# Ten pairs of projection tasks as block products with seven multiplications of blocks

## The chip, the cores and the metric
The kernel runs on one core of a Trainium2 chip. The metric is the device time of one execution in microseconds (us); lower is better. The engines are named as the profile names them: PE (TensorE, matmuls), PEld (its weight loads), DVE (VectorE), ACT (ScalarE), POOL (GpSimd) and SP (SyncE, which issues most of the DMAs). Each takes its instructions in order from a queue of its own.

## The reference
One step of a decoder layer for a prompt of 512 positions and 8 samples of 4 positions each, 544 columns in all (T), with a width of 1024.

```python
proj = jnp.einsum('btd,de->bte', x, p['w_in']) + p['b_in']
(q, k, v_a, o_a, z_a, i_pre, f_pre, u_b, v_b, z_b, x_c, z_c,
 g_a, g_b, g_c) = jnp.split(proj, _split_points(), axis=-1)
...
vn = layer_norm(v_b, p['gmlp_ln_g'], p['gmlp_ln_b'])
y_b = chunk_spatial_gate(u_b, vn, p['gmlp_ws'], p['gmlp_bs']) * jax.nn.silu(z_b)
...
merged = (jax.nn.sigmoid(g_a) * (y_a @ p['w_proj_a'])
          + jax.nn.sigmoid(g_b) * (y_b @ p['w_proj_b'])
          + jax.nn.sigmoid(g_c) * (y_c @ p['w_proj_c']))
out = merged @ p['w_out']
x_new = layer_norm(ALPHA * x + out, p['ln_g'], p['ln_b'])
```

y_a comes from four heads with a matrix memory, y_c from a gated linear recurrence (a scan over the positions). The change touches g_a, g_c and v_b.

## The kernel before
**Tasks.** Every projection is cut into tasks of 128 output channels (`proj`, `add`, run by `project`, L301). A task holds a 1024 x 128 block of weights as eight k-tiles of 128 x 128. The operands are fp32, and a matmul takes fp32r, so each operand is split into a high part (an ACT copy to fp32r) and a low part (a DVE subtraction): wh and wl for the weights (`need`, L255), xh and xl for the input. `products` adds wh·xh, wh·xl and wl·xh; T = 544 columns are two halves of 272, each in a PSUM bank of its own. A task is thus 8 x 3 x 2 = 48 matmuls. Its evacuation from PSUM is a function (`evac`): for the gates ga, gc one ACT tanh of 544 columns (gta, gtc), for pa a DVE multiplication by the gate that makes the merged sum mg, for vb an ACT copy with bias (vbt).

**Order.** The list of tasks is: the heads; xc0, zc0 to xc7, zc7 (the recurrence's inputs); ga0, ga1, pa0, pa1, ga2, ga3, pa2 and so on to pa7; the same with gc and pc; vb0 to vb7; zb0 to zb7; u0 to u7; gb and pb; then the output projection. PE, ACT, DVE and POOL take their instructions in the order in which the program records them. Work beside the tasks (the attention, the recurrence, `parts` which splits y_a into ya*h and ya*l for pa, `mixers`, `norm_v`) is written as generators: each yields a time or the name of something it waits for, and `poll`, called between groups of matmuls, lets each go on whose time has come by `clk`, a count of matmul time kept while recording. `force` drives them until a name in `gates` is done. So the recurrence of channel block 7 (tg7, a7, m7, the scan into xcv7, z_zc7) is recorded among the matmuls of ga0 to pa1, and `mixers` (nnps, lvps, lvo: states that go out, and masks) starts at vb1. `norm_v` transposes the finished vbt tiles into vt0, vt1 and so on for the layer norm.

**Buffers.** PSUM is split into `mm` (two buffers of two banks, the tasks' accumulators), `m2` (one buffer of two banks: lg, lvps, vt) and `aux` (two of one bank). A task's accumulator is free again when its `evac` has run. The weights wait in `wr` (two buffers of two tasks each, 1 MB, loaded from SP's queue), wh and wl have three buffers each.

Of the kernel before, what the change touches and what calls it, by code (L numbers as in the profile page):

```python
# [15 lines left out]
P = 128  # L16
# [25 lines left out]
def kernel(  # L42
# [227 lines left out]

    def products(i, k, ps):
        wh, wl = wts[i]
        vh, vl = tasks[i][4]()
        for n, (a, b) in enumerate(((wh, vh[k]), (wh, vl[k]), (wl, vh[k]))):
            for hf in range(2):
                matmul(ps[:, hf, :HT], a[:, k, :], b[:, hf * HT:(hf + 1) * HT],
                       start=(k == 0 and n == 0), stop=(k == KT - 1 and n == 2))
            if n < 2:
                poll()

    def project(first, last):
        for i in range(at[first], at[last] + 1):
# [3 lines left out]
            for _ in need(i):  # L286
                pass
            for _ in need(i + 1):
                pass
# [13 lines left out]
            poll()  # L303

# [92 lines left out]
    hrows = dr.tile([H, 2 * T + NS], F32, name="hrows")  # L397
    r_int = cp.tile([P, NS], F32, name="r_int")
# [166 lines left out]
    def add_head(h):  # L565
# [73 lines left out]
    def attention(h):  # L639
# [6 lines left out]
        bc = sp.tile([P, T + NS], F32, tag="bc", name=f"bc{h}", bufs=1)  # L646
# [62 lines left out]
        qp = sp.tile([P, 2, NS], F32, tag="qp", name=f"qp{h}", bufs=1)  # L709
# [44 lines left out]
        qt = sp.tile([P, 2, NS], F32, tag="qt", name=f"qt{h}", bufs=1)  # L754
# [77 lines left out]
        for dk in range(2):  # L832
# [8 lines left out]
            t_ = sp.tile([P, 258], F32, tag="cpo", name=f"cpo{h}{dk}", bufs=1)  # L841
# [171 lines left out]
    def add_merge(off, w, key, y):  # L1013
# [10 lines left out]
        vec = lambda: ([a for a, _ in ys], [b for _, b in ys])  # L1024

# [16 lines left out]

        for c in range(0, KT, 2):
# [11 lines left out]

    def ev_vb(c):
        def evac(ps):
            vbt[c] = slot("qk", f"vbt{c}")
            A.activation(h2(vbt[c]), p2(ps), AF.Identity, bias=bcol(O_VB + c * P)[0])
            if c == KT - 1:  # L1060
                go(norm_v())
        return evac
# [35 lines left out]
    def mixers():  # L1098
# [7 lines left out]
        nnr = sp.tile([P, 512], F32, tag="c0", name="nnr", bufs=4)[:36, :DK]  # L1106
# [9 lines left out]
        for hf in range(2):  # L1116
            t_ = sp.tile([P, 512], F32, tag="c0", name=f"lvo{hf}", bufs=4)
# [23 lines left out]
        mx.update(wmt=wmt, wsm2=wsm2, bsb=bsb)  # L1141

# [12 lines left out]
    def norm_v():  # L1155
        lng, lnb = [], []
        for hf in range(2):
            a = sp.tile([P, 512], F32, tag="c0h", name=f"glg{hf}", bufs=2)
            b = sp.tile([P, 512], F32, tag="c0l", name=f"glb{hf}", bufs=2)
# [5 lines left out]
        for i in range(NCH + 1):  # L1165
# [10 lines left out]
            for hf in range(2):  # L1176
                t_ = slot("kv", f"vn{i}{hf}") if i < NCH else sp.tile([P, 512], F32, tag="c0", name=f"vn{i}{hf}", bufs=4)
# [42 lines left out]
    def output():  # L1220
# [25 lines left out]
        for hf in range(2):  # L1246
# [6 lines left out]
            for oi, i in enumerate(orders[hf]):  # L1253
# [24 lines left out]
                if i == NCH:  # L1278
                    lo = sp.tile([P, 512], F32, tag="c0l", name=f"outl{hf}", bufs=2)
# [68 lines left out]
    gates["u0"] = ("vn",)  # L1348
# [6 lines left out]
    output()  # L1355
    assert not gens
# [30 lines left out]
```

## Time and profile before

| | us |
|---|---|
| median of 3 runs | 988.69 (984.44 to 989.75) |
| the profiled execution, its own time | 987.27 |
| its span, first to last instruction | 985.5 |
| PE busy | 972.1 (99%) |
| DVE busy | 549.8 (56%) |
| ACT busy | 412.3 (42%) |
| POOL busy | 97.5 (10%) |

The granted clock of PE was 0.992 of full speed on average. All times of the trace count from the start of the span. Ends of matmuls are modelled, so the time of one is read from the distance of many starts, as in the chain of waits, and not from the duration of one.

### The profile page before, as it was taken

The numbers are of one execution on the slowest core, as the hardware profiler recorded it, in microseconds if no ns is written. First come the engines' busy times: TensorE is split into PE (matmuls) and PEld (weight loads), VectorE is DVE, ScalarE is ACT, GpSimd is POOL, SyncE is SP. The second block draws the span as 40 slices with busy tenths as digits, with TensorE's granted clock in tenths as the row PEclk, the third lists the DMA queues.
The fourth block names the chain that finished last, engine by engine and source line by source line (L and its number), as shares of the span: only waits on it lengthen the run. The fifth ranks groups of instructions, "written<-read, shape, count | busy, mean of one in ns | idle before, by whom it ended". The sixth has DMA issues, their size and how long they took to land.

```text
span 985.5 us, 17775 instructions
## 1 busy us (share of the span) xinstructions
PE 972.1 (99%) x7433; PEld 948.7 (96%) x7433; DVE 549.8 (56%) x897; ACT 412.3 (42%) x653; POOL 97.5 (10%) x210
## 2 busy tenths in 40 slices
PE   8999999999999999999999999999999999999996
PEld 8999999999999999999999999999999999999975
DVE  4665675666567568889932243333167545433456
ACT  4454445445444545989922232222233213322421
POOL 5122002201200220001000000000000000000204
PEclk9999999999999999999999999999999999999998
DMA  8323721641462263233222222232223313431322
GB/s 252 101 63 120 214 80 61 192 131 50 133 195 86 60 195 105 77 96 92 87 86 88 91 84 95 95 109 70 88 84 97 102 63 99 140 107 43 102 65 101
DMA packets 101968, 103.55 MB, mean 105 GB/s; under 512 B 5358, under 2 KB 95320, under 8 KB 101888
## 3 DMA queue, kind: packets, MB, share of 16 engines
q1 hardware_dynamic: 100352, 101.46, 33.3%
q8 instruction: 58, 0.95, 0.4%
q10 hardware_dynamic: 640, 0.66, 0.2%
q0 software_dynamic: 896, 0.31, 0.1%
q14 instruction: 22, 0.18, 0.1%
HBM read 90.40 MB, written 12.00 MB: 104 GB/s over the span
## 4 chain that ended last, share of the span: by engine, by line
PE 98%; DMA 1%; issue 0%; ACT 0%; POOL 0%; DVE 0%; ACTq 0%; POOLq 0%
PE ps_v L96 5%; PE out L96 5%; PE ps_u L96 5%; PE ps_z L96 5%; PE ps_q L96 5%; PE ps_vb L96 5%; PE ps_zc L96 5%; PE ps_xc L96 5%; PE ps_pa L96 5%; PE ps_zb L96 5%; PE ps_ga L96 5%; PE ps_pc L96 5%; PE ps_k L96 5%; PE ps_o L96 5%; PE ps_gc L96 5%; PE ps_gb L96 5%
## 5 line engine op out<-in xcount | busy, mean ns | idle before, releaser
L795 DVE SCALAR_TENSOR_TENSOR c<-c,bc,cs 128x512 f32<-128x512 f32 x32 | 23.9, 746 | 36.2 <-PE cs L96 35.8
L777 POOL TENSOR_SCALAR wvm<-wvt,bm 96x256 fp32r<-96x256 f32 x32 | 31.5, 987 | 87.4 <-PE cs L96 87.4
L96 PE MATMUL ps_v<-xh,wh_v 128*128 128x272 f32 x128 | 29.1, 310 | 0.0
L774 ACT ACTIVATE c0h<-c 128x512 fp32r<-128x512 f32 x32 | 20.0, 625 | 21.6 <-DMA c<-in_state_mlstm_c_dram 20.1
L96 PE MATMUL ps_v<-xl,wh_v 128*128 128x272 f32 x128 | 28.1, 303 | 0.0
L96 PE MATMUL ps_v<-xh,wl_v 128*128 128x272 f32 x128 | 27.7, 299 | 0.0
L96 PE MATMUL ps_q<-xh,wh_q 128*128 128x272 f32 x128 | 27.3, 294 | 0.0
L96 PE MATMUL ps_u<-xh,wh_u 128*128 128x272 f32 x128 | 27.3, 294 | 0.0
L96 PE MATMUL ps_o<-xl,wh_o 128*128 128x272 f32 x128 | 27.1, 293 | 0.0
L96 PE MATMUL ps_z<-xh,wl_z 128*128 128x272 f32 x128 | 26.9, 291 | 0.0
L96 PE MATMUL ps_zb<-xh,wh_zb 128*128 128x272 f32 x128 | 26.8, 291 | 0.0
L96 PE MATMUL ps_o<-xh,wl_o 128*128 128x272 f32 x128 | 26.8, 291 | 0.0
L96 PE MATMUL ps_vb<-xh,wh_vb 128*128 128x272 f32 x128 | 26.8, 290 | 0.0
L96 PE MATMUL ps_z<-xh,wh_z 128*128 128x272 f32 x128 | 26.7, 290 | 0.0
L96 PE MATMUL ps_q<-xh,wl_q 128*128 128x272 f32 x128 | 26.7, 290 | 0.0
L96 PE MATMUL ps_q<-xl,wh_q 128*128 128x272 f32 x128 | 26.7, 289 | 0.0
L96 PE MATMUL ps_xc<-xl,wh_xc 128*128 128x272 f32 x128 | 26.6, 289 | 0.0
L96 PE MATMUL ps_gc<-xh,wh_gc 128*128 128x272 f32 x128 | 26.6, 288 | 0.0
L96 PE MATMUL ps_k<-xh,wl_k 128*128 128x272 f32 x128 | 26.6, 289 | 0.0
L96 PE MATMUL ps_gb<-xl,wh_gb 128*128 128x272 f32 x128 | 26.5, 289 | 0.0
L96 PE MATMUL ps_vb<-xh,wl_vb 128*128 128x272 f32 x128 | 26.5, 288 | 0.0
L96 PE MATMUL ps_zc<-xh,wh_zc 128*128 128x272 f32 x128 | 26.5, 289 | 0.0
(774 smaller groups left out, 3280.6 us busy)
## 6 DMA issues: line engine op xcount, KB each, us to landing
c<-in_state_mlstm_c_dram SPq DMA_DIRECT2D x32, 256.0 KB
out_dram<-c SPq DMA_DIRECT2D x32, 256.0 KB
wr_q<-in_w_in_dram SPq DMA_DIRECT2D x8, 512.0 KB
wr_k<-in_w_in_dram SPq DMA_DIRECT2D x8, 512.0 KB
wr_o<-in_w_in_dram SPq DMA_DIRECT2D x8, 512.0 KB
wr_z<-in_w_in_dram SPq DMA_DIRECT2D x8, 512.0 KB
wr_xc<-in_w_in_dram SPq DMA_DIRECT2D x8, 512.0 KB
wr_zc<-in_w_in_dram SPq DMA_DIRECT2D x8, 512.0 KB
```

Source lines behind the costliest of these rows:

```text
L96: PE.matmul(out, a, b, start=start, stop=stop)
L774: A.activation(hi[:, :512], t_[:, :512], AF.Copy)
L777: G.tensor_scalar(wvm, f(wvs), bm[:, b:b + 1], None, op0=ALU.mult)
L795: V.scalar_tensor_tensor(t_[:, :512], t_[:, :512], inter[:, DS * b + DS - 1:DS * b + DS], ps, op0=ALU.mult, op1=ALU.add)
```

## The change
ga4 to ga7, gc0 to gc7 and vb0 to vb7 are taken in pairs of neighbouring tasks, ten in all. A pair multiplies a 1024 x 256 block of weights with the 1024 x 544 input. `seven` sees it as 2 x 2 blocks: of the weights by halves of the k-tiles and by task, of the input by halves of the k-tiles and of the columns. It forms the four result blocks from seven block products (Winograd's form) in place of eight, each of 4 k-tiles, 3 parts and 272 columns: 84 matmuls in place of 96. The products go to three PSUM areas: X (four products), Y (two) and Z (one). `factors` makes the weights' block sums on DVE and splits them; `token_sums` makes the input's block sums once, from the time of ga0 on: t2, t3 and t4 into new tiles (40 DVE and 12 ACT operations of 128x272), and t1, after ga3, in place of one quarter of x (16 and 4). The quarter is saved to DRAM before (`spill`, eight DMAs of 139 KB) and brought back by `restore` after the last product that uses t1, in vb6. ga0 to ga3 and all other tasks stay as they were. `mixers` starts at zb0 and no longer at vb1; `norm_v` starts when the last vb pair ends. Small tiles move to a pool (`top`) whose memory is used again by the sums.

```diff
+    def units():
+        for i, t_ in enumerate(tasks):
+            if t_[0] in fast:
+                seq.extend((i, q) for q in range(4))
+            elif not (i and tasks[i - 1][0] in fast):
+                seq.append((i, None))
+        pos.update((u, n) for n, u in enumerate(seq))
...
+    def factors(i, q):
+        raw = load(i)
+        a11, a12, a21, a22 = (raw[:, 4 * k:4 * k + 4, m * P:(m + 1) * P] for m in range(2) for k in range(2))
+        wh = sp.tile([P, KT, P], F32R, tag="wh", name=f"wh_{tasks[i][0]}{q}", bufs=3)
+        wl = sp.tile([P, KT, P], F32R, tag="wl", name=f"wl_{tasks[i][0]}{q}", bufs=3)
+        wts[i, q] = (wh, wl)
+        def put(half, src):
+            ks = slice(4 * half, 4 * half + 4)
+            A.activation(wh[:, ks, :], src, AF.Copy)
+            V.tensor_tensor(wl[:, ks, :], src, f(wh[:, ks, :]), op=ALU.subtract)
+        if q == 0:
+            put(0, a11)
+            sums[i] = s3 = top[0].tile([P, 4, P], F32, tag="s3", name=f"s3_{i}", bufs=1)
+            V.tensor_tensor(s3, a11, a21, op=ALU.add)
+            yield
+            V.tensor_tensor(a21, a21, a22, op=ALU.add)
+            put(1, a21)
+        elif q == 1:
+            V.tensor_tensor(a21, a21, a11, op=ALU.add)
+            put(0, a21)
+            yield
+            put(1, a12)
+        elif q == 2:
+            put(0, sums[i])
+            yield
+            V.tensor_tensor(a21, a21, a12, op=ALU.add)
+            put(1, a21)
+        else:
+            put(0, a22)
...
+    def seven(i):
+        name = tasks[i][0]
+        dsts, bias, sc, func, finish = fast[name]
+        d0, d1 = dsts()
+        b0, b1 = bias
+        n0_ = pos[i, 0]
+        ps = mm(f"ps_{name}")
+        pz = aux(f"pz_{name}")
+        X, Y, Z = ps[:, 0, :HT], ps[:, 1, :HT], pz[:, :HT]
+        lo_, hi_ = slice(0, HT), slice(HT, T)
+        def q1():
+            A.activation(d0[:, lo_], X, AF.Identity, bias=b0, scale=sc)
+        def q5():
+            A.activation(d1[:, hi_], Y, AF.Identity, bias=b1, scale=-sc)
+        def q6():
+            A.activation(d0[:, hi_], X, AF.Identity, bias=b0, scale=sc)
+        def q2():
+            V.scalar_tensor_tensor(d0[:, lo_], Z, sc, d0[:, lo_], op0=ALU.mult, op1=ALU.add)
+        def q7():
+            V.scalar_tensor_tensor(d1[:, hi_], X, -sc, d1[:, hi_], op0=ALU.mult, op1=ALU.add)
+        def q3():
+            V.scalar_tensor_tensor(d0[:, hi_], Y, sc, d0[:, hi_], op0=ALU.mult, op1=ALU.add)
+        def q4():
+            A.activation(d1[:, lo_], X, func, bias=b1, scale=-sc)
+            if func != AF.Identity:
+                A.activation(d0[:, :T], d0[:, :T], func)
+                A.activation(d1[:, hi_], d1[:, hi_], func)
+        plan = ((0, 0, "b11", X, True, q1), (0, 1, "t1", Y, True, q5), (1, 0, "t2", X, False, q6), (1, 1, "b21", Z, True, q2),
+                (2, 0, "t3", X, False, q7), (2, 1, "b22", Y, False, q3), (3, 0, "t4", X, False, q4))
+        for q, half, tok, acc, first, after in plan:
+            wh, wl = wts[i, q]
+            for k in range(4):
+                th, tl = toks[tok][k]
+                ws_ = [w_[:, 4 * half + k, :] for w_ in (wh, wl)]
+                for n, (a, b) in enumerate(((ws_[0], th), (ws_[0], tl), (ws_[1], th))):
+                    matmul(acc, a, b, start=(first and k == 0 and n == 0), stop=(k == 3 and n == 2), more=not first)
+                if k == 0:
+                    prep(n0_ + q + 2, whole=bool(half) or q == 3)
+                    if q == 2 and half == 0 and i + 4 < len(tasks):
+                        load(i + 4)
+                poll()
+            after()
+            if tok == "t1" and name == last_fast:
+                restore()
+        finish()
+        done.update((name, tasks[i + 1][0]))
...
+            if name in fast:
+                seven(i)
+                i += 2
+                continue
...
+    def token_sums():
+        lo_, hi_ = slice(0, HT), slice(HT, T)
+        blk = {"b11": (0, lo_), "b12": (0, hi_), "b21": (4, lo_), "b22": (4, hi_)}
+        part = lambda b, k: tuple(x_[blk[b][0] + k][:, blk[b][1]] for x_ in (xh, xl))
+        for key, b in (("b11", "b11"), ("b21", "b21"), ("b22", "b22"), ("t1", "b12")):
+            toks[key] = [part(b, k) for k in range(4)]
+        for key in ("t2", "t3", "t4"):
+            toks[key] = []
+        def whole(k, b, tag):
+            t_ = top[0].tile([P, HT], F32, tag=tag, name=f"{b}{k}", bufs=1)
+            hi, lo = part(b, k)
+            V.tensor_tensor(t_, f(hi), f(lo), op=ALU.add)
+            return t_
+        def put(key, k, src, sign):
+            hi = top[0].tile([P, HT], F32R, tag="t", name=f"{key}h{k}", bufs=24)
+            lo = top[0].tile([P, HT], F32R, tag="t", name=f"{key}l{k}", bufs=24)
+            A.activation(hi, src, AF.Copy, scale=float(sign))
+            V.scalar_tensor_tensor(lo, src, float(sign), f(hi), op0=ALU.mult, op1=ALU.subtract)
+            toks[key].append((hi, lo))
+        for k in range(4):
+            for n, t_ in enumerate(part("b12", k)):
+                nc.sync.dma_start(spill[:, (2 * k + n) * HT:(2 * k + n + 1) * HT], f(t_))
+            a = whole(k, "b12", "ta")
+            b = whole(k, "b22", "tb")
+            yield 1.5
+            V.tensor_tensor(b, b, a, op=ALU.subtract)
+            put("t3", k, b, 1)
+            yield 1.5
+            a = whole(k, "b11", "ta")
+            V.tensor_tensor(a, a, b, op=ALU.add)
+            put("t2", k, a, -1)
+            yield 1.5
+            b = whole(k, "b21", "tb")
+            V.tensor_tensor(a, a, b, op=ALU.subtract)
+            put("t4", k, a, 1)
+            yield 1.5
+        if last_plain not in done:
+            yield last_plain
+        for k in range(4):
+            a = whole(k, "b11", "ta")
+            b = whole(k, "b12", "tb")
+            V.tensor_tensor(a, a, b, op=ALU.subtract)
+            hi, lo = part("b12", k)
+            A.activation(hi, a, AF.Copy)
+            V.tensor_tensor(lo, a, f(hi), op=ALU.subtract)
+            yield 0.7
+        done.add("toks")
+    def restore():
+        for k in range(4):
+            for n, x_ in enumerate((xh, xl)):
+                nc.sync.dma_start(f(x_[k][:, HT:T]), spill[:, (2 * k + n) * HT:(2 * k + n + 1) * HT])
...
+        def begin():
+            go(parts())
+            if key == "a":
+                next_top("tt")
+                go(token_sums())
...
+            if c >= quick:
+                fast[f"g{key}{c}"] = (gate_pair(c), [bcol(off + d * P)[1] for d in (c, c + 1)], 0.5, AF.Tanh, lambda: None)
             for d in (c, c + 1):
-                proj(f"g{key}{d}", off + d * P, ev_g(d), (lambda: go(parts())) if d == 0 and key != "b" else None)
+                proj(f"g{key}{d}", off + d * P, ev_g(d), begin if d == 0 and key != "b" else None)
...
-    add_merge(O_GA, w_pa[0], "a", ya)
-    add_merge(O_GC, w_pc[0], "c", yc)
+    add_merge(O_GA, w_pa[0], "a", ya, 4)
+    add_merge(O_GC, w_pc[0], "c", yc, 0)
+    last_plain, last_fast = "ga3", f"vb{KT - 2}"
+    gates["ga4"] = ("toks",)
...
+    def vb_end():
+        next_top("no")
+        go(norm_v())
...
-        proj(f"vb{c}", O_VB + c * P, ev_vb(c), (lambda: go(mixers())) if c == 1 else None)
+        if c % 2 == 0:
+            fast[f"vb{c}"] = (vb_pair(c), [bcol(O_VB + d * P)[0] for d in (c, c + 1)], 1.0, AF.Identity,
+                              vb_end if c == KT - 2 else lambda: None)
+        proj(f"vb{c}", O_VB + c * P, None)
     for c in range(KT):
-        proj(f"zb{c}", O_ZB + c * P, ev_zb(c))
+        proj(f"zb{c}", O_ZB + c * P, ev_zb(c), (lambda: go(mixers())) if c == 0 else None)
     for c in range(KT):
...
-    gates["u0"] = ("vn",)
+    gates["u0"] = ("vn", "mixers")
+    units()
```

**First place.** ACT, from the weights of pa0 to the evacuation gta0 of ga0, before:

```order
L267 ACTIVATE wh_pa0_5901<-wr_pa0_5818 128x1024
L552 ACTIVATE ya0h_5915<-ya0_1798 128x544
L552 ACTIVATE ya1h_5925<-ya1_1801 128x544
L552 ACTIVATE ya2h_5940<-ya2_2808 128x544
L976 ACTIVATE tg70_5955<-lg70_5948,gateb_169 128x284 x2
L552 ACTIVATE ya3h_5958<-ya3_2811 128x544
L552 ACTIVATE ya4h_5968<-ya4_3818 128x544
L1029 ACTIVATE gta0_5976<-ps_ga0_5882,vh__164 128x544
```

and now:

```order
L274 ACTIVATE wh_pa0_5915<-wr_pa0_5822 128x1024
L453 ACTIVATE t3h0_5922<-b220_5894 128x272
L739 ACTIVATE ya0h_5934<-ya0_1802 128x544
L739 ACTIVATE ya1h_5944<-ya1_1805 128x544
L453 ACTIVATE t2h0_5951<-b110_5948 128x272
L739 ACTIVATE ya2h_5966<-ya2_2812 128x544
L1163 ACTIVATE tg70_5981<-lg70_5974,gateb_172 128x284 x2
L739 ACTIVATE ya3h_5984<-ya3_2815 128x544
L453 ACTIVATE t4h0_5991<-b110_5948 128x272
L739 ACTIVATE ya4h_6001<-ya4_3822 128x544
L1222 ACTIVATE gta0_6009<-ps_ga0_5896,vh__167 128x544
```

Three copies of token sums (t3h0, t2h0, t4h0) stand ahead of gta0; each reads a tile (b220, b110) that DVE makes. Behind gta0 the same holds for t3h1, t2h1, t4h1 ahead of gta1.

**Second place.** DVE, from the low weights of ga2 to mg0, the evacuation of pa0, before:

```order
L268 TENSOR_TENSOR wl_ga2_6084<-wr_ga2_6018,wh_ga2_6083 128x1024
L997 SCALAR_TENSOR_TENSOR xcv7_5781<-a7_6027,m7_6028 128x568
L1004 SCALAR_TENSOR_TENSOR z_zc7_5877<-xcv7_5781,z_zc7_5877 128x512
L1006 SCALAR_TENSOR_TENSOR z_zc7_5877<-xcv7_5781,z_zc7_5877 128x32
L1036 SCALAR_TENSOR_TENSOR mg0_6128<-gta0_5976,ps_pa0_6070 128x544
```

and now:

```order
L275 TENSOR_TENSOR wl_ga2_6142<-wr_ga2_6057,wh_ga2_6141 128x1024
L447 TENSOR_TENSOR b122_6147<-xh2_84,xl2_92 128x272
L447 TENSOR_TENSOR b222_6149<-xh6_88,xl6_96 128x272
L1184 SCALAR_TENSOR_TENSOR xcv7_5785<-a7_6066,m7_6067 128x568
L1191 SCALAR_TENSOR_TENSOR z_zc7_5881<-xcv7_5785,z_zc7_5881 128x512
L1193 SCALAR_TENSOR_TENSOR z_zc7_5881<-xcv7_5785,z_zc7_5881 128x32
L463 TENSOR_TENSOR b222_6149<-b222_6149,b122_6147 128x272
L454 SCALAR_TENSOR_TENSOR t3l2_6172<-b222_6149,t3h2_6171 128x272
L447 TENSOR_TENSOR b112_6189<-xh2_84,xl2_92 128x272
L467 TENSOR_TENSOR b112_6189<-b112_6189,b222_6149 128x272
L454 SCALAR_TENSOR_TENSOR t2l2_6193<-b112_6189,t2h2_6192 128x272
L1229 SCALAR_TENSOR_TENSOR mg0_6204<-gta0_6009,ps_pa0_6128 128x544
```

Seven operations of the third k-tile's sums have come between, two of which read a copy of ACT's; 20 of the first two k-tiles stand further ahead.

**Third place.** PE and ACT where `mixers` starts. Before, at the end of vb0, on PE:

```order
L96 MATMUL ps_vb0_7802<-xh7_86,wl_vb0_7703 128x272 x2
L100 MATMUL nnps_7863<-ident_74,nn_158 36x128 x2
L100 MATMUL lvps_7869<-ident_74,lv_182 36x128 x8
L96 MATMUL ps_vb1_7884<-xh0_79,wh_vb1_7757 128x272 x2
L96 MATMUL ps_vb1_7884<-xl0_87,wh_vb1_7757 128x272 x2
L96 MATMUL ps_vb1_7884<-xh0_79,wl_vb1_7758 128x272 x2
```

and on ACT:

```order
L267 ACTIVATE wh_vb2_7815<-wr_vb2_7761 128x1024
L1059 ACTIVATE vbt0_7855<-ps_vb0_7802,vb__163 128x544
L1118 ACTIVATE lvo0_7878<-lvps_7869 36x512
L267 ACTIVATE wh_vb3_7897<-wr_vb2_7761 128x1024
L1118 ACTIVATE lvo1_7918<-lvps_7869 36x512
L1059 ACTIVATE vbt1_7946<-ps_vb1_7884,vb__163 128x544
```

Now, at the end of the last vb pair, on PE (seven more transposes into vt0 follow, then zb0):

```order
L103 MATMUL ps_vb6_8407<-t4l3_6312,wh_vb63_8453 128x272
L103 MATMUL ps_vb6_8407<-t4h3_6311,wl_vb63_8454 128x272
L107 MATMUL nnps_8548<-ident_77,nn_161 36x128 x2
L107 MATMUL lvps_8554<-ident_77,lv_186 36x128 x8
L107 MATMUL vt0_8569<-ident_77,vbt0_8030 128x128
```

and on ACT:

```order
L274 ACTIVATE wh_zb1_8516<-wr_zb0_8356 128x1024
L377 ACTIVATE vbt7_8406<-ps_vb6_8407,vb__166 128x272
L1312 ACTIVATE lvo0_8563<-lvps_8554 36x512
L274 ACTIVATE wh_zb2_8602<-wr_zb2_8487 128x1024
L1312 ACTIVATE lvo1_8612<-lvps_8554 36x512
L747 ACTIVATE t_zb0_8653<-ps_zb0_8586,vh__167 128x544
```

lvps and vt0 are both in `m2`, and now follow each other at once; vt0 waits for lvo1, which stands behind wh_zb2.

## Rows read from the trace of the kernel before

**Rows 1.** page, parts 1 and 4: busy time by engine; shares of the chain
```profile
PE 972.1 (99%) x7433; PEld 948.7 (96%) x7433; DVE 549.8 (56%) x897; ACT 412.3 (42%) x653; POOL 97.5 (10%) x210
...
PE 98%; DMA 1%; issue 0%; ACT 0%; POOL 0%; DVE 0%; ACTq 0%; POOLq 0%
```

**Rows 2.** chain of waits, 440 to 720: start us, us, what
```profile
484.02 12.08 PE ps_pa L96 x96
496.10 12.06 PE ps_ga L96 x96
...
664.91 6.02 PE ps_vb L96 x48
```

**Rows 3.** busy time by windows: engines (x instructions), clock, DMA share, GB/s
```profile
470.00:482.00 12.00, 12.00 (x98) 12.00 (x97) 11.20 (x17) 11.96 (x20) 0.83 (x2) 1.00 0.29 89
482.00:494.00 12.00, 12.00 (x98) 12.00 (x97) 11.79 (x21) 8.95 (x11) 1.67 (x4) 1.00 0.27 89
494.00:506.00 12.00, 12.00 (x98) 12.00 (x97) 4.85 (x5) 2.72 (x3) 0.00 (x0) 1.00 0.29 87
688.70:700.80 12.10, 12.10 (x99) 12.10 (x98) 2.45 (x2) 3.32 (x4) 0.00 (x0) 1.00 0.29 88
```

**Rows 4.** DVE timeline, 474 to 497: start, us, engine, line, operation [idle <-releaser]
```profile
475.20 0.72 DVE L562 SCALAR_TENSOR_TENSOR z_zc<-t_zc,z_zc 128x544 f32<-128x544 f32 x1 [0.61 <-ACT z_zc L561]
475.85 0.74 DVE L989 SCALAR_TENSOR_TENSOR m<-a,m 128x568 f32<-128x568 f32 x1
...
478.50 1.23 DVE L268 TENSOR_TENSOR wl_pa<-wr_pa,wh_pa 128x1024 fp32r<-128x1024 f32 x1
479.64 0.72 DVE L553 TENSOR_TENSOR ya0l<-ya,ya0h 128x544 fp32r<-128x544 f32 x1
480.27 0.72 DVE L553 TENSOR_TENSOR ya1l<-ya,ya1h 128x544 fp32r<-128x544 f32 x1
480.91 1.34 DVE L997 TENSOR_TENSOR_SCAN xcv<-a,m 128x568 f32<-128x568 f32 x1
...
493.83 0.71 DVE L1036 SCALAR_TENSOR_TENSOR mg<-gta,ps_pa 128x544 f32<-128x544 f32 x1
...
496.14 0.72 DVE L1036 SCALAR_TENSOR_TENSOR mg<-gta,ps_pa 128x544 f32<-128x544 f32 x1 [0.46 <-PE ps_pa L96]
```

**Rows 5.** ACT timeline, 474 to 497
```profile
475.06 1.06 ACT L267 ACTIVATE wh_pa<-wr_pa 128x1024 fp32r<-128x1024 f32 x1
476.01 0.65 ACT L552 ACTIVATE ya0h<-ya 128x544 fp32r<-128x544 f32 x1
...
479.51 0.73 ACT L1029 ACTIVATE gta<-ps_ga,vh__164 128x544 f32<-128x544 f32 x1
...
488.40 0.72 ACT L1029 ACTIVATE gta<-ps_ga,vh__164 128x544 f32<-128x544 f32 x1
```

**Rows 6.** groups by line and form, 460 to 716: busy us, mean ns | idle
```profile
L945 DVE TENSOR_TENSOR lw<-lwr,lw 128x256 fp32r<-128x256 f32 x1 | 0.4, 426 | 0.0
...
L987 ACT ACT_TABLE_LOAD x3 | 3.8, 1283 | 0.1
```

**Rows 7.** ACT timeline, 670 to 676
```profile
672.06 0.59 ACT L1118 ACTIVATE lvo<-lvps 36x512 f32<-36x512 f32 x1 [0.38 <-PE lvps L100]
672.56 1.05 ACT L267 ACTIVATE wh_vb<-wr_vb 128x1024 fp32r<-128x1024 f32 x1
673.50 0.58 ACT L1118 ACTIVATE lvo<-lvps 36x512 f32<-36x512 f32 x1
```

**Rows 8.** SP's queue, timelines at 19 and 675: two loads in a row
```profile
19.34 0.92 SPq L252 DMA_DIRECT2D wr_k<-in_w_in_dram  x2
...
675.72 0.96 SPq L252 DMA_DIRECT2D wr_vb<-in_w_in_dram  x2
```

**Rows 9.** busy time by windows near the start
```profile
4.00:7.00 3.00, 1.59 (x13) 1.07 (x11) 0.76 (x2) 1.23 (x3) 1.87 (x4) 1.00 1.16 307
8.00:11.00 3.00, 3.00 (x16) 3.00 (x15) 1.99 (x6) 1.80 (x7) 2.68 (x7) 0.50 1.13 356
```

More of the change, by code (lines that the diff above doesn't have):

```diff
@@ L59, with next_top @@
     dr = ctx.enter_context(tc.tile_pool(name="dr", bufs=1, space=bass.MemoryType.DRAM))
+    top = [tc.alloc_tile_pool(name="at", bufs=1, reuse_waits="tile")]
+    def next_top(name):
+        top[0].release()
+        top[0] = tc.alloc_tile_pool(name=name, bufs=1, reuse_waits="tile")
     def slot(tag, name, dt=F32):
@@ L91, with matmul @@
     gens = []
-    def matmul(out, a, b, start, stop):
+    def matmul(out, a, b, start, stop, more=False):
         cols = math.prod(b.shape[1:])
         clk[0] += cols / 2400 if b.dtype == F32R and cols >= 256 else max(cols, 16) / 600
-        PE.matmul(out, a, b, start=start, stop=stop)
+        PE.matmul(out, a, b, start=start, stop=stop, skip_group_check=more)
     def transpose(out, a, idn):
@@ L269, in need, with prep @@
             yield
+    fast, seq, pos = {}, [], {}
+    def units():
[5 more added lines that the diff above has]
+        pos.update((u, n) for n, u in enumerate(seq))
+    sums, preps = {}, {}
+    def factors(i, q):
[27 more added lines that the diff above has]
+            put(0, a22)
+            yield
+    def prep(n, whole=True):
+        if n >= len(seq):
+            return
+        if n not in preps:
+            i, q = seq[n]
+            preps[n] = need(i) if q is None else factors(i, q)
+        if whole:
+            for _ in preps[n]:
+                pass
+        else:
+            next(preps[n], None)
     def products(i, k, ps):
@@ L281, in project @@
     def project(first, last):
-        for i in range(at[first], at[last] + 1):
+        i = at[first]
+        while i <= at[last]:
             name, w2d, off, c, vec, evac, pre = tasks[i]
@@ L285, in project @@
                 force(g)
[L286 to L289, printed above, removed]
+            n0_ = pos[i, 0 if name in fast else None]
+            prep(n0_)
+            prep(n0_ + 1)
             if pre:
                 pre()
+            if name in fast:
+                seven(i)
+                i += 2
+                continue
             ps = mm(f"ps_{name}")
@@ L295, in project @@
                 if k == 1:
-                    for _ in need(i + 2):
-                        pass
+                    prep(n0_ + 2)
                     if i + 3 < len(tasks):
@@ L413, in gate @@
         for q in range(2):
-            w_ = sp.tile([P, 512], F32R, tag="c0", name=f"wg{q}", bufs=4)
+            w_ = top[0].tile([P, 512], F32R, tag="c0", name=f"wg{q}", bufs=4)
             wg.append(w_.rearrange("p (k c) -> p k c", k=4))
@@ L644, in attention @@
         yield f"values{h}"
-        bc = sp.tile([P, T + NS], F32, tag="bc", name=f"bc{h}", bufs=1)
+        bc = top[0].tile([P, T + NS], F32, tag="bc", name=f"bc{h}", bufs=1)
         nc.sync.dma_start(bc, hrows[h:h + 1, 0:T + NS].to_broadcast([P, T + NS]))
@@ L706, in keys @@
                 kw.append(t_)
[L709 removed]
+        qp = top[0].tile([P, 2, NS], F32, tag="qp", name=f"qp{h}", bufs=1)
         V.tensor_tensor(qp, qs, inter[:, None, :].to_broadcast([P, 2, NS]), op=ALU.mult)
@@ L840, in attention @@
                     i += 1
-            t_ = sp.tile([P, 258], F32, tag="cpo", name=f"cpo{h}{dk}", bufs=1)
+            t_ = top[0].tile([P, 258], F32, tag="cpo", name=f"cpo{h}{dk}", bufs=1)
             A.activation(t_[:, :257], ps[:, :257], AF.Copy)
@@ L1041, in ev_p, with gate_pair, dsts @@
             return evac
+        def gate_pair(c):
+            def dsts():
+                for d in (c, c + 1):
+                    tg[d] = slot("dm", f"gt{key}{d}")
+                return tg[c], tg[c + 1]
+            return dsts
         for c in range(0, KT, 2):
+            if c >= quick:
+                fast[f"g{key}{c}"] = (gate_pair(c), [bcol(off + d * P)[1] for d in (c, c + 1)], 0.5, AF.Tanh, lambda: None)
             for d in (c, c + 1):
-                proj(f"g{key}{d}", off + d * P, ev_g(d), (lambda: go(parts())) if d == 0 and key != "b" else None)
+                proj(f"g{key}{d}", off + d * P, ev_g(d), begin if d == 0 and key != "b" else None)
             for d in (c, c + 1):
@@ L1054 @@
     mx = {}
[L1056 to L1062, printed above, removed]
     def ev_zb(c):
@@ L1116, in mixers @@
         for hf in range(2):
-            t_ = sp.tile([P, 512], F32, tag="c0", name=f"lvo{hf}", bufs=4)
+            t_ = top[0].tile([P, 512], F32, tag="c0", name=f"lvo{hf}", bufs=4)
             A.activation(t_[:36, :512], lo_[:36, hf, :], AF.Copy)
@@ L1141, in mixers @@
         mx.update(wmt=wmt, wsm2=wsm2, bsb=bsb)
+        done.add("mixers")
     def ln_stats(stt, n, name):
@@ L1355 @@
     output()
+    top[0].release()
     assert not gens
```

54 lines of the change are left out of this document (32 added, 22 removed).

## Prediction
> **What bounds the kernel now.** I read the page first: PE is busy 972.1 us of 985.5 and stands on 98% of the chain that ended last, DVE 549.8 and ACT 412.3 [rows 1]. So matmuls that go away pay, unless something makes PE wait. The chain of waits over the tasks that change says what a matmul costs: 96 of ps_ga take 12.06 us, 48 of ps_vb take 6.02 [rows 2]; that is 125.6 ns each, with no gap between tasks. Then I asked where DVE and ACT have room, by windows [rows 3]. In the vb stretch DVE works 2.45 us of 12.1; but from 470 to 494, while PE runs ga0 to pa1, it works 22.99 of 24, and ACT 11.96 of the first 12. The timelines of that stretch [rows 4, 5] show two queues that are barely in time: DVE's only idle time from 475 to 495 is 0.61 us before z_zc, mg (the evacuation of pa0) starts at 493.83 and ends at 494.54, and PE can take ga2 at 496.10 [rows 2] only because pa0's accumulator is then free. That is 1.6 us of slack. The recording order says that pa0 and pa1 take the accumulators that gta0 and gta1 (ACT) give back, and ga2 and ga3 those of mg0 and mg1 (DVE); there are two.
>
> **Part 1: fewer matmuls.** Each of ten pairs does 7 products of 4 k-tiles in 3 parts, 84 matmuls of 272 columns, where two tasks did 96. 10 x 12 x 125.6 ns = **15.07 us** less PE, all of it on the path [rows 1, 2]. The Trainium skill, "TensorE: Matmul & The Clock Gate", section "Back-to-back issue gap", gives N/2.4 + 2.5 ns for a single matmul at full clock, 115.8 ns here: an estimate by it would be 13.9 us, and the sum 1.2 us higher. The trace has a duration for just this matmul and decides.
>
> **Part 2: the token sums, beside ga0 to ga3.** From ga0 on, 40 DVE operations and 12 ACT copies of 128x272 are put between the work of rows 4 and 5. An operation of 272 columns: 256 columns take 0.43 us and 1024 take 1.22 [rows 6, 4], so 272 take 0.44; consecutive operations overlap by 0.09 (0.72 long, 0.63 apart in the ya rows [rows 4]), so 0.36 in a row, about 0.47 where one needs the one before. An ACT copy is about 0.35 in a row (ya0h, 544 columns, 0.65 [rows 5]).
> Throughput alone: 27 of the DVE operations stand ahead of mg0, 27 x 0.36 = 9.7, less the slack of 1.6: **8.1 us** that ga2 would be late. But the queues also wait for each other: each t-copy on ACT needs a sum of DVE's, and each remainder on DVE needs that copy; and gta0, gta1 stand behind the copies on ACT (order, first place). Replaying the two orders with the rows' durations:
> - t3h0 stands where ya0h began, at 476.01. Its sum b220 comes on DVE after z_zc at 475.20, two sums, the m chain and wl_pa (478.50 and 479.64 were their ends [rows 4]), now 0.72 later: ready at 480.8. ACT idles 4.8 us. t2h0 then waits to 484.0, and t4h0 to 488.9 (scan of 1.34, two products, two ya remainders ahead of its sum).
> - gta0, at 479.51 before, ends at about 490.8. pa0, at 484.02 before [rows 2], starts there: 6.8 late. It would end at 496.9.
> - gta1, at 488.40 before [rows 5], now stands behind ya5h to ya7h, wh_pa, a, m, a table load of 1.28 [rows 6] (to 497.5), t3h1 (497.9), t2h1 (499.3), then the m7 chain on DVE (2.65, as in [rows 4]: 475.85 to 478.50) before t4h1 (503.7), and a table load. It ends at 506.0: pa1 is 9.2 later still.
> - mg0 needs t3, t2 of k = 2, wl_ga2, scan and z_zc ahead of it (order, second place): it ends at 514.7, when pa1 is done at 512.1: 2.6 more. mg1, one weight remainder and 11 operations on, ends at 522.7 against 520.7: 2.0 more.
> Sum **20.6 us**, range 16 to 21 by how much of the handovers overlap; below it stands the 8.1 of throughput alone, above it nothing that I find, since after ga3 the queues have room (4.85 of 12 us of DVE from 494 on [rows 3]). I take the replay, because both queues are in order and rows 4 and 5 leave no room to absorb it. PE's waits of 7 and 9 us may lower the clock: after a stretch with PE busy 1.59 of 3 us, 3 us ran at 0.50 [rows 9], 1.5 us lost; here this falls into the waits for gta1 and mg0, so I add nothing.
> The sums that overwrite x (16 on DVE, 4 copies, beside pa2 and pa3, about 16 x 0.4 = 6.4 of 12 us) fit.
>
> **Part 3: the boundary from vb to zb.** mixers() moves to zb0, and norm_v starts in the same instant. Its first transposes (vt0) write the one two-bank accumulator that lvps holds until lvo0 and lvo1 have left on ACT, and between these now stands wh_zb2 (order, third place). Before, PE went on with vb1 meanwhile and nobody waited. lvo 0.59, wh 1.05, lvo 0.58 [rows 7] in a row: **2.2 us** of PE, 0.5 if wh finds itself behind, 3.5 if wr_zb2 lands late. That load is issued behind the eight DMAs that bring x back, 139 KB each. Those start after the t1 product of vb6, 60 matmuls or 7.5 us ahead of zb0; at 0.48 us each to issue [rows 8] and 356 GB/s [rows 9] they take 3.8 + 3.1 = 6.9: hidden, with little over. The eight that save x stand on SP ahead of wr_k, which before left only at 19.34 [rows 8], after x was made: nothing.
>
> **Part 4: the pairs themselves.** A pair needs 7 weight remainders and 4 sums of 128x512 on DVE (about 0.69 each by [rows 4, 6], 0.6 in a row) and 3 evacuations: 8 of 10.55 us, where 2.45 of 12.1 were used; ACT about 6. PE goes back to the same bank three times a pair, with 12 matmuls (1.5 us) of another bank in between for the evacuation of 0.42. That covers one weight operation ahead of it, not three. I take 0.3 at each border between vb pairs and 0.5 at gc0: **1.4**, range 0 to 15 (30 returns of 0.5). The Trainium skill, "Perfetto Trace Analysis", section "Matmuls" under "Optimizing Tensor Performance", speaks against this part: independent groups of matmuls should rotate through different banks, so that one is emptied under the next; the plain tasks do so, as the gapless chain shows. By it, the stall below would be the likelier; no row of before shows a return to a bank so soon.
>
> **Sum.** The profiled execution took 987.27 (span 985.5), 1.4 under the median of 988.69. 987.27 - 15.07 + 20.6 + 2.2 + 1.4 = **996.4**.
>
> **Rivals.**
> - Throughput only: 987.27 - 15.07 + 8.1 + 2.2 + 1.4 = 983.9. For it: DVE and ACT both have enough time in total after 497. Against it: it needs gta0 and gta1 early, and both stand behind copies that wait for DVE.
> - Faster, the sums hidden: 987.27 - 15.07 + 2.2 + 1.4 = 975.8. For it: PE is the bound by far, and DVE idle 44% of the span. It decides at gta0: if that ends before about 485, pa0 is on time. Against it: 22.99 busy of 24.
> - The pairs stall at their banks on top: 996.4 - 1.4 + 15 = 1010. For it: three returns a pair behind DVE's weight work. Against it: DVE and ACT are each below 80% there.
> That the change saves fewer matmuls than it says is excluded by the order, which has 84 a pair.
>
> **How the numbers follow.** The replay (991 to 1003) has 0.60, throughput only 0.17, sums hidden 0.12, pairs stalled 0.11. No change is within 0.5% of the median, 983.7 to 993.6, about what a measurement of this kernel can tell. Faster: all of the hidden case and half of the throughput case (0.08), 0.20. Within: the other 0.09 and 0.13 of the replay at its short end, 0.22. Slower: the rest, 0.58. The range leaves out the hidden case and most of the stalls: 979 to 1004.
>
> **What would show it.** 84 matmuls a pair in 10.6 us; PE idle ahead of pa0 and pa1, ended by ACT's gta, and ahead of ga2, ga3, ended by DVE's mg; ACT idle in front of t3h0, t2h0, t4h0; PE idle about 2 us ahead of vt0, ended by lvo. It is wrong if pa0 starts before 487, or if the pairs take much more than 11 us.

## The result
The changed kernel takes 1040.13 us (median of 4 runs, 1039.97 to 1040.38) against 989.18 for the kernel before (4 runs): slower, by a factor of 1.0526 (95% interval 1.0494 to 1.0559). The forecast was 996.4 with a range of 979 to 1004. The direction was right, the size was not: the time is 36 us beyond the upper end.

The page of the profile after, its parts 1 and 4, to be held beside [rows 1]:

```profile
PE 976.6 (94%) x7313; PEld 943.0 (91%) x7313; DVE 632.4 (61%) x1073; ACT 450.5 (43%) x751; POOL 97.6 (9%) x210
...
PE 85%; DVE 7%; ACT 6%; issue 1%; DMA 1%; POOL 0%; SPq 0%; POOLq 0%; ACTq 0%; DVEq 0%
```

PE's share of the chain fell from 98% to 85%; DVE and ACT now stand on it with 13%. What PE waited for, over the whole span (us in total, times, longest):

```profile
PE ps_pa L103 <- ACT gta L1222: 13.4, 2, 6.8
PE ps_gc L103 <- DVE gtc L371: 6.2, 4, 2.6
PE ps_vb L103 <- DVE vbt L371: 3.7, 4, 1.2
PE ps_ga L103 <- DVE mg L1229: 3.0, 3, 1.8
PE ps_gc L103 <- ACT gtc L362: 2.5, 4, 0.6
PE ps_ga L103 <- DVE gta L371: 2.4, 2, 1.2
PE ps_gc L103 <- ACT gtc L359: 2.3, 4, 0.6
PE ps_vb L103 <- ACT vbt L362: 2.3, 4, 0.6
PE ps_vb L103 <- ACT vbt L359: 2.3, 4, 0.6
PE ps_vb L103 <- DVE vbt L374: 2.3, 4, 0.6
PE ps_gc L103 <- DVE gtc L374: 2.1, 4, 0.5
PE vt L107 <- ACT lvo L1312: 2.1, 1, 2.1
PE ps_ga L103 <- ACT gta L362: 1.7, 2, 1.0
PE ps_ga L103 <- ACT gta L359: 1.5, 2, 0.9
...
PE ps_ga L103 <- DVE gta L374: 1.1, 2, 0.5
```

Three kinds stand there. gta (L1222) and mg (L1229) are the waits ahead of pa0, pa1 and ga2 to ga4; vt for lvo is the boundary from vb to zb; both were forecast. The other twelve rows are new. Their lines are in `seven`: L359 is q1, L362 q5, L371 q7 and L374 q3, the evacuations of b11, t1, t3 and b22. All ten pairs have all four, 40 waits, 30.4 us.

The stretch that was replayed, on PE (start, us; in brackets the idle time and what ended it):

```profile
491.51 0.59 PE L103 MATMUL ps_pa<-ya0h,wh_pa 128*128 128x272 f32 x1 [6.79 <-ACT gta L1222]
...
506.80 0.60 PE L103 MATMUL ps_pa<-ya0h,wh_pa 128*128 128x272 f32 x1 [6.66 <-ACT gta L1222]
...
515.59 0.36 PE L103 MATMUL ps_ga<-xh,wh_ga 128*128 128x272 f32 x1 [0.89 <-DVE mg L1229]
...
523.60 0.36 PE L103 MATMUL ps_ga<-xh,wh_ga 128*128 128x272 f32 x1 [1.75 <-DVE mg L1229]
```

and on ACT, ahead of gta0, where [rows 5] show no gap:

```profile
481.52 0.43 ACT L453 ACTIVATE t3h<-b 128x272 fp32r<-128x272 f32 x1 [4.69 <-DVE b L463]
...
484.75 0.43 ACT L453 ACTIVATE t2h<-b 128x272 fp32r<-128x272 f32 x1 [1.71 <-DVE b L467]
...
489.88 0.43 ACT L453 ACTIVATE t4h<-b 128x272 fp32r<-128x272 f32 x1 [2.84 <-DVE b L471]
...
490.77 0.69 ACT L1222 ACTIVATE gta<-ps_ga,vh__167 128x544 f32<-128x544 f32 x1
```

The three copies wait for DVE's sums, as the order of the queues said, and gta0 stands behind them.

Then one pair, gc6 and gc7, on PE: the last matmul ahead of the first wait, and the first matmul after each of the four:

```profile
681.51 0.29 PE L103 MATMUL ps_gc<-xh,wl_gc 128*128 128x272 f32 x1
682.38 0.39 PE L103 MATMUL ps_gc<-xh,wh_gc 128*128 128x272 f32 x1 [0.58 <-ACT gtc L359]
...
684.80 0.39 PE L103 MATMUL ps_gc<-t2h,wh_gc 128*128 128x272 f32 x1 [0.64 <-ACT gtc L362]
...
690.75 0.39 PE L103 MATMUL ps_gc<-xh,wh_gc 128*128 128x272 f32 x1 [1.19 <-DVE gtc L371]
...
693.06 0.39 PE L103 MATMUL ps_gc<-t4h,wh_gc 128*128 128x272 f32 x1 [0.53 <-DVE gtc L374]
```

At 682.38 PE begins t1, which goes to Y, and waits for q1, which empties X. At 684.80 it begins t2, into X, and waits for q5, which empties Y; the same at 690.75 (Y after q7 of X) and 693.06 (X after q3 of Y). Each product waits for the evacuation of the product just ended, though that one is in the other bank. From start to start the first wait takes 0.87 us where 0.13 is due.

The sum by stages, of which each start is that of a stage's first matmul (ga0 starts at 470.23 before and 470.94 after):

| stage | before | after | more |
|---|---|---|---|
| ga0 to the start of ga4 | 49.84 | 71.35 | 21.5 |
| ten pairs (plain: 10 x 12.06, [rows 2]) | 120.6 | 147.8 | 27.2 |
| pc0 and pc1 | 12.06 | 13.09 | 1.0 |
| wait ahead of vt0 | 0 | 2.1 | 2.1 |

Together 51.8; the spans from ga0 on differ by 52.0 (515.3 and 567.3). The pairs' 27.2 are 42.3 of waits less 15.1 of matmuls saved. The 42.3 are the 30.4 that the rows name, by estimate some 0.25 more at each of 40 restarts, and the lowered clock at gc0 (1.7, below).

### The profile page after: what moved, and what is told of

The parts are those of the page before. It is cut to its first block, busy times and chain, and to the rows that moved or that the text cites. A ratio compares the mean times of both kernels' runs of the same rounds, so it can differ in the third digit from the quotient of the medians.

```text
span 1038.3 us, 17864 instructions
## 1 busy us (share of the span) xinstructions
PE 976.6 (94%) x7313; PEld 943.0 (91%) x7313; DVE 632.4 (61%) x1073; ACT 450.5 (43%) x751; POOL 97.6 (9%) x210
## 4 chain that ended last, share of the span: by engine, by line
PE 85%; DVE 7%; ACT 6%; issue 1%; DMA 1%; POOL 0%; SPq 0%; POOLq 0%; ACTq 0%; DVEq 0%
PE ps_v L103 5%; PE out L103 5%; PE ps_u L103 5%; PE ps_pc L103 5%; PE ps_z L103 5%; PE ps_q L103 5%; PE ps_zb L103 5%; PE ps_o L103 5%; PE ps_k L103 5%; PE ps_gb L103 5%; PE ps_pb L103 5%; PE ps_xc L103 4%; PE ps_zc L103 4%; PE ps_gc L103 3%; PE ps_vb L103 3%; PE ps_pa L103 2%
## 5 line engine op out<-in xcount | busy, mean ns | idle before, releaser
L302 DVE TENSOR_TENSOR wl_gc<-wr_gc,wh_gc 128x512 fp32r<-128x512 f32 x24 | 16.3, 691 | 21.8 <-ACT wh_gc L301 21.8
L103 PE MATMUL ps_ga<-xh,wh_ga 128*128 128x272 f32 x88 | 20.8, 295 | 6.9 <-DVE mg L1229 3.0
L103 PE MATMUL ps_o<-xl,wh_o 128*128 128x272 f32 x128 | 27.2, 293 | 0.0
L103 PE MATMUL ps_zb<-xh,wl_zb 128*128 128x272 f32 x128 | 26.9, 291 | 0.0
L103 PE MATMUL ps_zb<-xl,wh_zb 128*128 128x272 f32 x128 | 26.6, 289 | 0.0
```

The source lines that it names most:

```text
L103: PE.matmul(out, a, b, start=start, stop=stop, skip_group_check=more)
L302: V.tensor_tensor(wl[:, ks, :], src, f(wh[:, ks, :]), op=ALU.subtract)
```

## The experiments
Where ga0 starts differs by up to 5.7 us between the runs (see the last section), so the runs are compared by the span from ga0 on, 567.3 for the changed kernel. Each is one execution, but for the last two, which have six.

**own_y: Y in a tile of its own.**

```diff
+        py = aux(f"py_{name}")
         pz = aux(f"pz_{name}")
-        X, Y, Z = ps[:, 0, :HT], ps[:, 1, :HT], pz[:, :HT]
+        X, Y, Z = ps[:, 0, :HT], py[:, :HT], pz[:, :HT]
```

> Edit: the area Y of a pair gets a PSUM tile of its own (one bank of aux) where it was the second bank of X's tile. Theory A: X and Y are one tile to the program's bookkeeping, so PE waits ahead of t1, t2, b22 and t4 for the evacuation of the product just ended although it writes the other bank. Then the four waits (30.4 us over ten pairs as the trace names them, about 36 with the restart of the matmul stream) go: pairs fall from 14.2 to about 10.6 us and the time from 1040.1 to 1004 (1001 to 1009). Rival B (the prediction's stall rival): PE comes back to the same bank too soon and the evacuations stand behind weight work on DVE and ACT; X is still used four times, so the waits ahead of t2 and t4 stay, and only those of t1 and b22 could shrink: 1020 or more.

Measured: 1003.43 us in one run; 529.0 from ga0 on, 38.3 less. Of the twelve rows two are left (L360 and L372 are q1 and q7 here):

```profile
PE ps_pa L103 <- ACT gta L1223: 13.7, 2, 6.9
PE ps_ga L103 <- DVE mg L1230: 3.3, 3, 1.8
PE vt L107 <- ACT lvo L1313: 2.1, 1, 2.1
PE ps_gc L103 <- DVE gtc L372: 1.7, 1, 1.7
...
PE ps_vb L103 <- ACT vbt L360: 0.9, 3, 0.3
```

The chain of waits of that run, the pair gc2 and gc3 (start, us, what):

```profile
614.31 1.50 PE ps_gc L103 x12
615.81 1.49 PE py_gc L103 x12
617.30 1.50 PE ps_gc L103 x12
...
623.29 1.50 PE ps_gc L103 x12
624.79 12.06 PE ps_pc L103 x96
```

10.48 us for 84 matmuls, without a gap; the ten pairs fell from 147.8 to 109.0. Theory A holds, with 38.3 us less where it had 36. That the time came within 1 us of its 1004 is in part luck: ga0 began 1.7 us later than in the changed kernel. B falls: X is still used four times, and 1.5 us of another area is cover enough. What remains (q7 at gc0 behind the splits of y_c, q1 at the borders of the vb pairs) is 2.6 us in all.

**copies_on_dve: the copies of the sums from ACT to DVE.**

```diff
-            A.activation(hi, src, AF.Copy, scale=float(sign))
+            V.tensor_scalar(hi, src, float(sign), None, op0=ALU.mult)
```

> Edit: the twelve copies of the token sums go from ACT to DVE; nothing else. DVE then has 52 operations of 128x272 where it had 40, and no queue waits for another's sums. Theory (the two queues wait for each other): gta0 and gta1 are back in time, pa0 and pa1 start without the waits of 6.8 and 6.7; ga2 is late by the 36 operations ahead of mg0, 36 x 0.36 - 1.6 = 11.4; the slip falls from 21.4 to about 13 and the time to 1031. Rival (throughput alone: what counts is DVE's time): 12 operations more, slip 25.7, 1044. The clock's falls before ga0 differ from run to run, so the verdict is read from ga0 on.

Measured: 1032.72; 561.0 from ga0 on, 6.3 less. pa0 starts on time, ga2 is late:

```profile
483.58 0.42 PE L103 MATMUL ps_pa<-ya0h,wh_pa 128*128 128x272 f32 x2
...
508.13 0.57 PE L103 MATMUL ps_ga<-xh,wh_ga 128*128 128x272 f32 x1 [8.67 <-DVE mg L1229]
```

DVE has 12 operations more and the stretch is shorter. So the copies ahead of gta0 and gta1 caused the waits ahead of pa0 and pa1, and DVE's work alone, which would have made the slip longer, does not explain it. But of the slip of 21.5 only 6.4 went; the rest has moved to DVE's queue. The stretch from ga0 to ga4 is 64.95, a slip of 15.1 where 13 was expected: pa0 waited 2.7 for its parts of y_a besides, and ga2 and ga3 took 14.2 for 12.06, partly at a lowered clock (0.86 from 510 to 520).

**late_sums: the sums begin after the recurrence.**

```diff
     def token_sums():
+        if "lru7" not in done:
+            yield "lru7"
...
-            yield 1.5
+            yield 1.2
```

> Edit: the token sums begin when the recurrence's last block is done (lru7), 1.2 in place of 1.5 apart; Y still shares X's tile. Theory (queues that wait for each other, copies ahead of gta0 and gta1): pa0 and pa1 start with no wait, 16 us less; ga2 and ga3 still 1 to 2 late each, since t3 and t2 of k = 0 stand ahead of mg0; and the sums end up to 7 later than ga4 wants them. 1040.1 - 21 + 2 to 9: 1021 to 1028. Rival (throughput: DVE simply lacks the time): the slip moves to ga2 to ga4 and stays at 15 or more: 1034 or more.

Measured: 1029.65; 559.7 from ga0 on, 7.7 less. The time lies between the two, the slip does not: from ga0 to ga4 it is 65.9 us, a slip of 16.0, as the rival had it. The time is below the rival's 1034 because ga0 began 2.7 us earlier, and because the clock did not fall at gc0, which is worth 2.7; neither lies in the stretch that the edit changes. pa0 and pa1 have no wait, but mg2 (mg3 in the expectations of sums_on_pool and nine_pairs_yc) is late behind the sums:

```profile
496.60 0.53 PE L103 MATMUL ps_ga<-xh,wh_ga 128*128 128x272 f32 x2 [2.49 <-DVE mg L1231]
...
534.12 0.57 PE L103 MATMUL ps_ga<-xh,wh_ga 128*128 128x272 f32 x1 [8.40 <-DVE mg L1231]
```

The 56 operations do not fit between the recurrence and ga4: the first pair comes too soon. DVE's busy time alone is not what is missing, though. The remainder of a sum stands in DVE's queue right behind the sum and waits for ACT's copy of it, 16 times 0.5 us, 7.9 in all; two of them:

```profile
509.66 0.44 DVE L456 SCALAR_TENSOR_TENSOR t3l<-b,t3h 128x272 fp32r<-128x272 f32 x1 [0.50 <-ACT t3h L455]
...
511.42 0.44 DVE L456 SCALAR_TENSOR_TENSOR t2l<-b,t2h 128x272 fp32r<-128x272 f32 x1 [0.49 <-ACT t2h L455]
```

That is nearly the whole wait of 8.4 ahead of ga4. Whether other work put between a sum and its remainder would have saved it is open.

**later_vt: the transposes after some matmuls of zb0** (`yield 3.0` at the head of norm_v).

> Edit: norm_v yields 3 us before its first transposes, so they are recorded after some 24 matmuls of zb0. Theory: the wait of 2.1 us for lvo goes, 1038.0 (1037.5 to 1038.5). Rival: vt0 or a later vt waits for something else, 1040.

Measured: 1033.65; 564.9 from ga0 on, 2.4 less. The wait is gone: PE does 28 matmuls of zb0 between lvps and vt0. The other 4 us of the difference, by which the time lies below its range, lie ahead of ga0 and are not the edit's.

**all_three: the three edits together.**

> The three edits together. If the causes add up: 1040.1 - 36 - (12 to 19) - 2 = 983 to 990, at or just under the kernel before. If they cover each other (a wait removed here uncovers one there), 995 or more.

Measured: 994.86; 520.7 from ga0 on, 46.6 less, where the three runs alone sum to 38.3 + 7.7 + 2.4 = 48.4. They add up to within 2 us, and the clock that did not fall at gc0 is counted in two of the three; the total is above the range because late_sums brought less. It is still slower than the kernel before (987.97 beside it): the 13.5 us of waits for mg and gta that are left take most of what the matmuls save.

**sums_on_pool: all three, with the 24 plain sums on POOL** (`V.tensor_tensor` to `G.tensor_tensor` in `whole`).

> As the run of all three edits with ten pairs, but the 24 plain sums (high + low of one block) go from DVE to POOL. There mg3 stood 8.4 us late behind sums on DVE. If DVE's time was what lacked: 24 x 0.36 = 8.6 us less on DVE and 994.9 falls to 986 (984 to 989). If POOL's operation (wvm of 96x256 takes 0.99 us) holds DVE and ACT up instead: 995 or more.

Measured: 998.0, as the second of the two expectations had it. The wait ahead of ga4 grew from 8.4 to 10.8. A sum takes 0.93 us there and 0.43 on DVE (b, L449, in late_sums), and DVE waits 8.3 us for them (the last two rows, from DVE's waits), about what it was to save:

```profile
L450 POOL TENSOR_TENSOR b<-xh,xl 128x272 f32<-128x272 f32 x24 | 22.0, 929 | 20.0 <-DVE t4l L457 8.3 <-DVE xl L485 6.3 <-DVE b L470 3.2
...
DVE b L482 <- POOL b L450: 4.7, 3, 1.6
DVE b L466 <- POOL b L450: 3.6, 4, 1.6
```

**eight_pairs: the sums spread, the first pair at gc0.** own_y and later_vt with

```diff
     def token_sums():
+        if "pa1" not in done:
+            yield "pa1"
...
-            yield 1.5
+            yield 3.0
...
-    add_merge(O_GA, w_pa[0], "a", ya, 4)
+    add_merge(O_GA, w_pa[0], "a", ya)
...
-    last_plain, last_fast = "ga3", f"vb{KT - 2}"
-    gates["ga4"] = ("toks",)
+    last_plain, last_fast = "ga7", f"vb{KT - 2}"
+    gates["gc0"] = ("toks",)
```

> Y in its own tile, the later vt, and ga4 to ga7 plain again, so that the token sums can be spread from pa1 to pa7 (3 us apart) and the first pair is gc0. If the three causes are all there is: 8 x 12 x 0.1256 = 12.1 us fewer matmuls against the kernel before, less 1.7 at gc0 (yc parts ahead of q7 on DVE), 1 at the borders of vb and up to 1 for the sums: 988 - 12.1 + 3.5 = 979 (976 to 983), faster than the kernel before. If the pairs or the sums cost PE time of another kind: 985 or more.

Measured: 983.73, the kernel before beside it 989.57. From ga0 on 509.0, 6.3 less than the kernel before, where 12.1 less 3.5 was expected; the time is just above the range, with ga0 2.4 us later than in the kernel before. The sums cost 0.4 (mg, ahead of gc0), but gc0 waits 1.8 (for q6) and 0.3 (for q7), and right behind the first wait the clock fell to 0.50 (580 to 582), which took another 1.7.

**eight_pairs_yc: and the splits of y_c 1.0 apart.**

> As eight_pairs, with the eight splits of y_c spread over gc0 (1.0 apart, not 0.48), so that fewer stand ahead of the evacuations q6 and q7 there. Theory (an evacuation that stands behind other work in its queue is what is left of the pairs' cost): the waits of 1.8 and 0.3 at gc0 go, and with them the clock's fall after them: 96 x 0.1256 = 12.1 less 0.9 (vb borders) and 0.4 (mg): 10.5 to 11 us under the kernel before, 978, ratio 0.989. Rival (the gain is smaller than the matmuls' count for a reason still unseen): 982 or more.

Measured: 980.76 (6 runs) against 988.78 (11 runs), ratio 0.9919 (0.9903 to 0.9935). Faster than before by 0.8%, which is small but clear of the interval. The theory did not hold: the waits at gc0 did not go, q6 and q7 are 1.2 late each, 2.4 where it was 2.0. The clock did not fall there this time, and that is enough for the 1.1 us by which the span from ga0 on is shorter (507.9). Beside the splits, the weights of this first pair stand ahead of q6: ACT was idle 1.78 us until 573.17 for their block sum (wr_gc, on DVE), and then had two weight copies, q5 and two splits to do before q6 at 575.70, though t2 had ended at 573.5.

**nine_pairs_yc: ga6 and ga7 a pair too**, the sums 1.5 apart, gate at ga6.

> As eight_pairs_yc with ga6 and ga7 a pair too: the sums stand 1.5 apart from pa1 on and end with pa5. DVE has 30 us from pa1 to ga6 for 56 operations (20) and eight weight remainders (9) and four mg (3), 32 in all: nearly full. If that fits: 108 x 0.1256 = 13.6 less 1.3, about 976.5, ratio 0.9875. If mg4 or mg5 stand late behind the sums, as mg3 did with ten pairs: 1 to 3 us of wait ahead of ga6, 978 to 981.

Measured: 978.93 (973.61 to 979.19, 6 runs) against 988.78, ratio 0.989 (0.9871 to 0.9909). It beats both kernels. The sums fit, so the first case of the expectation is the right one: mg makes ga6 wait 0.4 and not 1 to 3 us. The median lies 2.4 above that case all the same; four of the six runs took 978.8 to 979.2 at a granted clock of 0.992, the other two 976.37 (the profiled one) at 0.994 and 973.61 at 0.996. What PE still waited for around the change (L1232 is mg, L360 q1, L372 q7):

```profile
PE ps_vb L103 <- ACT vbt L360: 0.9, 3, 0.3
...
PE ps_gc L103 <- DVE gtc L372: 0.6, 1, 0.6
PE ps_ga L103 <- DVE mg L1232: 0.4, 1, 0.4
```

From ga0 on it takes 504.6, 10.7 less than before. 108 matmuls at 0.1256 are 13.6; of the 2.9 that are missing 1.9 are these waits. At gc0, no longer the first pair, q6 is not late.

## Why the prediction was wrong
**Part 1, 15.07 us of matmuls: right.** In own_y a pair takes 10.48 where two tasks took 12.06: 1.58 each, 15.8 in ten. The matmul of the pairs runs at 124.8 ns. The 115.8 that the Trainium skill, "TensorE: Matmul & The Clock Gate", section "Back-to-back issue gap", gives for a single matmul is not reached in this trace.

**Part 2, the token sums, 20.6: right,** step by step. Waits ahead of pa0 and the later ones, forecast and measured: 6.8 and 6.9; 9.2 and 9.2 (6.7 of idle, and pa0 itself slower at the lowered clock); 2.6 and 2.8; 2.0 and 2.0. ACT's idle ahead of t3h0: 4.8 and 4.7. The stretch lost 21.5, of which 0.5 at ga4. Copies_on_dve and late_sums show that the copies ahead of gta0 and gta1 caused the waits ahead of pa0 and pa1, as the replay had it. They also show that the 8.1 of throughput alone was too low: with these copies out of the way the slip is still 15.1 and 16.0.

**Part 3, 2.2: right,** 2.1; later_vt took it away. lvo, wh_zb2 and lvo on ACT were what stood in between, with the durations of [rows 7]. Bringing x back was hidden: zb0's first matmul waits for nothing but vt0 ahead of it.

**Part 4, 1.4 with 15 as its upper end: wrong, measured 42.3.** The step that failed is "PE goes back to the same bank three times a pair, with 12 matmuls (1.5 us) of another bank in between for the evacuation". X and Y are two banks, but one tile (`ps`), and in this program a write to a tile is ordered behind the read of it that was recorded before, whichever half that one reads; own_y shows it. So the cover of 1.5 us was there for Z alone, and four products of seven waited for the evacuation recorded just before them, 0.53 to 2.63 us each. DVE's load, which the part weighed, was as forecast (8.35 of 11.2 us in own_y's first vb pair) and not the cause: it is the same work in own_y, where the waits are gone. The tile could have been read from the code: one `mm` call, two areas cut from it. The plain tasks use the same tile without harm because both halves are emptied at once.

**The rivals.** The stall rival (1010) had the right place and the wrong cause: it had returns to the same bank behind DVE's weight work. The Trainium skill, "Perfetto Trace Analysis", section "Matmuls" under "Optimizing Tensor Performance", says that independent groups should rotate through different banks, so that one is emptied under the next. X, Y and Z do lie in different banks in this kernel; what stopped the rotation was the tile. With one tile per area, X's bank is returned to just as soon and shows no such wait but at gc0 and at the borders of the vb pairs. The part's upper end was built from that rival with 0.5 for each of 30 returns; it was 40 waits, at 1.06.

## What to carry to other kernels
An accumulator that is emptied by itself needs a tile by itself: where two areas of one tile are written and read in turn, each write waits for the other area's reader, and ten pairs lost 38 us to it. Work that is put beside the main line is to be replayed against the queues' order with the rows' durations before it is priced by throughput: here that gave four waits to 0.2 us, and showed copies that wait for another engine holding up the evacuation behind them. To take them away brought 6 of 21.5 us back; what brought the rest was more time for the sums. And a saving of an eighth of the matmuls of a stretch came out only after its preparation was moved to where DVE had room: nine pairs with the sums spread (978.93) beat ten with the sums crowded (994.86).

## What the runs showed of the hardware
**The clock falls in places where PE is fully busy,** and not in the same ones each time. own_y has three such stretches ahead of ga0 (at 116, 202 and 372), the kernel before two between 20 us and ga0 (at 200 and 285), later_vt one (at 282); windows of PE (start:end, length, busy, clock, DMA share, GB/s), of own_y:

```profile
116.00:118.00 2.00, 2.00 (x11) 0.50 0.80 165
```

and of the kernel before:

```profile
284.00:286.00 2.00, 2.00 (x10) 0.53 0.25 69
```

The first one of own_y takes 0.89, 0.50 and 0.76 in three windows of 2 us, 1.7 us lost. With other differences of the start such falls move ga0 between 466.99 (later_vt, one fall) and 472.69 (sums_on_pool, three). That is as much as several of the edits, and why they were compared from ga0 on.

**After the same wait the clock fell in one run and not in another.** At gc0 of the changed kernel PE stood still from 605.6 to 608.27, and then:

```profile
606.00:608.00 2.00, 0.00 (x0) 1.00 0.27 94
608.00:610.00 2.00, 1.73 (x12) 0.85 0.00 0
610.00:612.00 2.00, 1.47 (x6) 0.50 0.03 8
```

The half clock, 1.2 of 2.4 GHz, is why pc0 and pc1 take 13.09 there. In late_sums PE stood still as long at the same place, and the clock stayed:

```profile
600.69 0.39 PE L103 MATMUL ps_gc<-xh,wh_gc 128*128 128x272 f32 x1 [2.63 <-DVE gtc L371]
...
602.00:604.00 2.00, 1.47 (x12) 1.00 0.00 0
604.00:606.00 2.00, 2.00 (x18) 1.00 0.06 17
```

The 2.1 us ahead of vt0 are another such case: the clock was at 0.50 from 730 to 732 in own_y, right behind them, and stayed at 1.00 in the changed kernel. So in these runs a wait of this length does not decide by itself whether the clock falls. In the other pairs of the changed kernel, with waits of 0.5 to 1.2 us, the clock stayed at 1.00.
